# Hybrid decoder block on one core: va, z, gate, branch and output products turned from 256 moving activations to 512 moving weight columns

## The chip, the cores and the metric

One Trainium2 chip, of which the kernel uses one core (core 0). The metric is the device time of one execution in microseconds (us), as a median of several runs. The engines are named as in the profile: PE is TensorE, DVE VectorE, ACT ScalarE, POOL GpSimd, SP the queue that issues most transfers.

## The reference

One decoder block on 256 tokens of 1024 channels, all in float32. Norm weights, the convolution and the decay parameters are left out here.

```python
h = rmsnorm(x, pre_norm_w)
proj = h @ w_in                       # 1024 x 10256
q_a, k_a, v_a, z_a, q_b, k_b, v_b, z_b, beta, decay, gate_a, gate_b = split(proj)
o_a = attention(rope(q_a), rope(k_a), v_a)          # causal softmax, 8 heads of 128
y_a = (o_a * silu(z_a)) @ w_branch_a
q_b, k_b, v_b = split(silu(causal_dwconv(concat(q_b, k_b, v_b))))
o_b = rmsnorm(gated_deltanet(q_b, k_b, v_b, g, beta))   # 8 heads, chunked delta rule
y_b = (o_b * silu(z_b)) @ w_branch_b
merged = sigmoid(gate_a) * y_a + sigmoid(gate_b) * y_b
return x + rmsnorm(merged @ w_out, post_norm_w)
```

With 256 tokens the attention has a single block of keys, so it is plain causal attention.

## The kernel before, in words

**Products.** Every large product is made in three single passes over a split of its operands: each float32 operand is cut into a part `hi` that the fast matmul type (float32r) holds exactly and a rest `lo`, and the product is hi*hi + hi*lo + lo*hi. The weights come as 104 tiles of 512 KB, 128 output columns of all 1024 rows each (`slots`, line 291; `load`, line 319). For each tile `prep` (line 328) has ACT write `hi` (L341), then DVE or, for some tiles, POOL write `lo` (L344 to L346), and then issues the load of the tile five places on, into one of five buffers.

- `projT` (line 376) takes the 128 weight columns as the stationary operand and lets the 256 tokens of the normalised input (`Hh`, `Hl`: hi and lo, channels on partitions) move: 24 matmuls 128x256 for a tile, accumulated in one PSUM tile (`psP`, three of them). The result has channels on partitions, tokens along the row. It serves qb, kb, vb, qa, ka, za, zb, ga, gb and the branch products wa, wb.
- `projN` (line 388) does it the other way for va and the output product wo: 128 tokens stationary, 256 weight columns moving, so a pair of tiles gives two PSUM tiles of 24 matmuls.

**Order of the tiles.** kb, qb, va in pairs; qa, vb, ka in pairs; then eight tiles each of za, zb, ga, gb; then wa and wb in turn; then wo. In what follows dl is the PSUM tile of a head of the delta rule, s that of a head of the attention, kk that of `unit`, vT, oT those of transposes, po that of the output product.

**Order of everything else.** Each engine executes in the order in which the program emits. The tile loop (line 1013) emits the products, and between every three matmuls `tick` (line 198) lets side tasks emit their next stage: `conv` and `unit` (products of a head), `inverses` (DVE: 62 operations on the tile `NtTt`, then a round trip through DRAM as `dT` into the tile `DT`), `head` (the delta rule, starts when `DT` is there), `ybtask`, `att`, `merge`. A stage is emitted when a running estimate of each engine's clock (`clk`, line 60) says that its operands are there; the estimate of a fast matmul is line 128: `max(0.107, size(out) / 2350.0)` us.

**Gates and merge.** `zgate` (line 743) makes z * (1 + tanh(z/2)) by channels. `ybtask` (line 832) scales a head's output per token on DVE, transposes it on PE to channels, gates it from PSUM, and `hilo` (line 819) splits it with ACT and POOL. `att` (line 898) does scores, softmax, transposes of the probabilities, the product with va as the stationary operand, so that its result has channels on partitions, then gate and split. wa and wb then let these tiles move. `merge` (line 948) adds on POOL, and ACT and DVE split into `mH`, `mL`.

**End.** `final` (line 980) is called for each half of the tokens (t) and each 256 columns (n): ACT sums squares, DVE multiplies the PSUM tile by the norm weight; after the last n, eight tiny DVE operations (`ro`) make the reciprocal root, then three DVE (or ACT and POOL) operations add the residual and three transfers write the row.

**Buffers.** `big` has nine tiles of 8 KB a partition, `dp` 24 of 2 KB; PSUM has three banks in `psP` and five in `psM`, which the side tasks take and give back.

Of the kernel before, what the change touches and what calls it, by code (L numbers as in the profile page):

```python
# [37 lines left out]
def tile_moba_gdn_block(  # L38
# [111 lines left out]
    big = ctx.enter_context(tc.tile_pool(name="big", bufs=9))  # L150
    dp = ctx.enter_context(tc.tile_pool(name="dp", bufs=24))
# [21 lines left out]
    left = {"d": [0.0] * 24, "w1": [0.0] * 8, "E": [0.0] * 2}  # L173
# [125 lines left out]

    for n in range(4):  # L300
        pair("kb", KB, n)
        pair("qb", QB, n)
        pair("va", VA, n)
# [13 lines left out]
    raws, wts, natw = {}, {}, {}  # L317

    def load(i, t=None):
        if i < NS:  # L320
            kind, n, src, c0 = slots[i]
            r = wp.tile([P, KT, P], F32, tag="raw", bufs=5, name=f"raw{i}")
            at(clk["T"] if t is None else t)
            dma(nc.sync, r, src.rearrange("(k p) c -> p k c", p=P)[:, :, c0:c0 + P])
            raws[i] = r
            done(f"raw{i}")

    def prep(i, now=False, pool=None):
# [3 lines left out]
        if kind in ("va", "wo"):  # L332
            if (kind, n // 2) not in natw:
                natw[kind, n // 2] = [bigt(f"{kind}{w}{n}", F32R).rearrange("p (k c) -> p k c", k=KT) for w in "hl"]
            c = slice((n % 2) * P, (n % 2) * P + P)
            hi, lo = (a[:, :, c] for a in natw[kind, n // 2])
        else:
            hi = wp.tile([P, KT, P], F32R, tag="hi", name=f"hi{i}")
            lo = wp.tile([P, KT, P], F32R, tag="lo", name=f"lo{i}")
            wts[i] = (hi, lo)  # L340
# [18 lines left out]
    def palloc(name):  # L359
# [6 lines left out]
        ps = psP.tile([P, S], F32, tag="pj", name=name)  # L366
# [9 lines left out]
    def projT(i, rh, rl, name):  # L376
        hi, lo = wts.pop(i)
        ps = palloc(name)
# [9 lines left out]
    def projN(lh, ll, t, wh, wl, name):  # L388
        ps = palloc(name)
        c = 0  # L390
        for k in range(KT):
            for a, b in ((lh, wh), (ll, wh), (lh, wl)):
                T.matmul(ps, a(k)[:, t * P:(t + 1) * P], b[:, k, :], start=(c == 0), stop=(c == 3 * KT - 1))
                c += 1
                if c % 3 == 0 and c < 24:
                    tick()
        return ps

# [65 lines left out]
    first = [palloc(f"pkb{n}") for n in range(2)]  # L464
# [22 lines left out]
    # every product starts as soon as its column and its weights are there  # L487
# [37 lines left out]
    def betadecay():  # L525
# [8 lines left out]
        # beta = 1 / (1 + exp(-b))  # L534
# [3 lines left out]
        # softplus(z) = max(z, 0) + log1p(exp(-|z|))  # L538
# [17 lines left out]
        # cumulative sums over each chunk of 128 tokens, as rows and per token  # L556
# [105 lines left out]
    def factors(g):  # L662
# [10 lines left out]
        # eps * 128 * (|q2|^2 + 4 eps)  # L673
# [66 lines left out]
    zs = [None] * H  # L740
    zsuse = [0] * H

    def zgate(dst, ps, name):
        pid = pids[0] - 1
        th = tmp.tile([P, S], F32, tag="w1", bufs=8, name=f"thz{name}")
        act(th, ps, AF.Tanh, scale=0.5)
        yield
        V.scalar_tensor_tensor(dst, th, 1.0, ps, op0=OP.add, op1=OP.mult)
        pfree(pid)
        free("w1")  # L750
        done(f"z{name}")

# [66 lines left out]
    def hilo(y, src):  # L819
        act(y[:, 0, :], src, AF.Copy)  # L820
        G.tensor_tensor(y[:, 1, :], src, f(y[:, 0, :]), op=OP.subtract)

# [9 lines left out]
    def ybtask(h):  # L832
        yield from need(f"rf{h // 4}", f"zb{h}")
        yield from until(lambda: yrun[0] < 2)
        yrun[0] += 1
        ps = yield from take(f"oT{h}")
        Vs = AV[h][:, 1]
        for t in range(NT):
            u = t * 8 + h
            V.tensor_scalar(Vs[:, t, :], Vs[:, t, :], sm[:, F_, u:u + 1], None, op0=OP.mult)  # L840
        yield
        for t in range(NT):
            T.transpose(ps[:, t * P:(t + 1) * P], Vs[:, t, :], ident)
        yield
        yield from room("w1")
        y = tmp.tile([P, S], F32, tag="w1", bufs=8, name=f"yb_{h}")
        V.scalar_tensor_tensor(y, ps[:, 0:S], gdnw, zs[h][:, 0, :], op0=OP.mult, op1=OP.mult)
        give()
        zsuse[h] += 1
        free("d", 1 + (zsuse[h] == 2))  # L850
        yield from room("d")
        yb[h] = dt_(f"yb{h}", F32R)
        hilo(yb[h], y)
        free("w1")
# [43 lines left out]
    def att(h):  # L898
        yield from need("rope", f"za{h}")
# [19 lines left out]
        V.reciprocal(mx[:, 6:8], mx[:, 4:6])  # L919
        for t, (a, b) in enumerate(ab):  # L920
            V.tensor_scalar(p[:, a:b], p[:, a:b], mx[:, 6 + t:7 + t], None, op0=OP.mult)
        yield
# [3 lines left out]
        act(pe, ps[:, 0:384], AF.Copy)  # L926
        yield
# [5 lines left out]
        y = tmp.tile([P, S], F32, tag="w1", bufs=8, name=f"ya_{h}")  # L933
        V.scalar_tensor_tensor(y, ps[:, 0:256], 0.5, zs[h][:, 1, :], op0=OP.mult, op1=OP.mult)
# [233 lines left out]
```

## Time and profile before

| | |
|---|---|
| median of 3 runs | 405.76 us (404.92 to 408.33) |
| span of the profiled execution | 403.9 us |
| PE busy | 376.6 us, 93% |
| DVE busy | 306.5 us, 76% |
| ACT busy | 199.5 us, 49% |
| POOL busy | 130.6 us, 32% |
| moved by DMA | 64.20 MB, mean 159 GB/s |

The page gives the profiled execution by its span, from the first to the last instruction, and no separate time; the median of the timed runs lies 1.9 us above the span, and that is taken for what lies around it. A busy share is an average over stages. A line of the chain of waits gives start, length and the group that the end was waiting for at that time. A line of the timeline gives the start of the first of a few equal instructions and the time to the end of the last; a matmul's end is modelled and overlaps the next, so the pace of matmuls is read from the distance of starts. All matmuls go through one helper and stand under line 129, transposes under 133, other operations under 117, transfers under 147; they are told apart by tile names.

### The profile page before, as it was taken

To read this page: it belongs to the slowest core of one execution; us is meant where nothing else is said; L and a number is where in the kernel's file an instruction comes from. 1 tells how busy PE (TensorE), PEld (TensorE's weight loads), DVE (VectorE), ACT (ScalarE), POOL (GpSimd) and SP (SyncE) were. 2 spreads that over 40 slices of the span, in tenths; PEclk is the share of its full clock that TensorE was granted. 3 is DMA by queue.
4 is the path that set the end of the run, shared out by engine and by line. 5 is a ranking of instruction groups with operands and counts; after the bars stand their busy time and mean duration, and the time that the engine had idled before them with its cause. 6 is when DMAs were issued, how large, how long until landed. Compare 5 with 4: busy or idle time off the path is not lost.

```text
span 403.9 us, 7830 instructions
## 1 busy us (share of the span) xinstructions
PE 376.6 (93%) x3011; PEld 369.6 (92%) x3011; DVE 306.5 (76%) x664; ACT 199.5 (49%) x429; POOL 130.6 (32%) x102
## 2 busy tenths in 40 slices
PE   6799999959999899789999999999999999999992
PEld 5699999859999899689999999999999999999992
DVE  4869879997959699999966684776988543769645
ACT  3357456534564555435534545654757543444411
POOL 2540447463764453312055001011232201446101
PEclk9699999978999999969999999999999999999998
DMA  8964948543455795346898723342365466577402
GB/s 236 283 157 107 249 132 231 145 133 104 109 154 150 188 286 147 107 126 173 248 288 212 191 57 102 84 102 77 93 169 157 137 195 193 165 229 211 128 0 104
DMA packets 119447, 64.20 MB, mean 159 GB/s; under 512 B 6514, under 2 KB 117987, under 8 KB 119411
## 3 DMA queue, kind: packets, MB, share of 16 engines
q1 hardware_dynamic: 116578, 60.42, 54.8%
q0 software_dynamic: 736, 2.24, 1.6%
q10 hardware_dynamic: 2096, 1.06, 0.9%
q8 instruction: 23, 0.38, 0.4%
q14 instruction: 14, 0.11, 0.1%
HBM read 61.08 MB, written 2.63 MB: 158 GB/s over the span
## 4 chain that ended last, share of the span: by engine, by line
PE 72%; DVE 21%; issue 4%; DMA 1%; ACT 1%; DVEq 0%; SPq 0%; ACTq 0%
PE dl L129 7%; PE po L129 6%; PE pza L129 6%; PE pgb L129 6%; PE pga L129 6%; PE pzb L129 6%; PE pwa L129 5%; PE pwb L129 5%; PE pkb L129 5%; DVE lo L117 4%; DVE NtTt L117 4%; PE pqb L129 4%; PE pvb L129 4%; PE pva L129 3%; PE s L129 3%
## 5 line engine op out<-in xcount | busy, mean ns | idle before, releaser
L117 DVE TENSOR_TENSOR lo<-raw,hi 128x1024 fp32r<-128x1024 f32 x74 | 102.7, 1394 | 10.9 <-ACT hi L117 10.8
L117 ACT ACTIVATE hi<-raw 128x1024 fp32r<-128x1024 f32 x88 | 92.3, 1052 | 19.9 <-PE pwb L129 10.6
L117 POOL TENSOR_TENSOR lo<-raw,hi 128x1024 fp32r<-128x1024 f32 x14 | 34.0, 2432 | 45.7 <-ACT hi L117 45.7
L117 DVE TENSOR_TENSOR NtTt<-NtTt 128x112 f32<-128x112 f32 (+27 forms) x62 | 34.2, 552 | 1.6
L117 POOL TENSOR_TENSOR ya<-ya,ya 128x256 fp32r<-128x256 f32 x8 | 8.5, 1064 | 76.3 <-ACT ya L117 76.3
L117 POOL TENSOR_TENSOR val<-raw,vah 128x1024 fp32r<-128x1024 f32 x8 | 19.6, 2455 | 21.8 <-ACT vah L117 21.8
L129 PE MATMUL pwa<-ya,hi 128*128 128x256 f32 x128 | 23.4, 283 | 0.0
L129 PE MATMUL pwb<-yb,hi 128*128 128x256 f32 x128 | 23.4, 283 | 0.0
L117 POOL TENSOR_TENSOR my<-my,m 128x256 f32<-128x256 f32 x8 | 10.4, 1295 | 33.1 <-DVE my L117 33.1
L129 PE MATMUL pzb<-Hh,hi 128*128 128x256 f32 x64 | 20.8, 325 | 0.0
L129 PE MATMUL pga<-Hh,hi 128*128 128x256 f32 x64 | 20.2, 315 | 0.0
L129 PEld LDWEIGHTS pwb<-yb,hi 128*128 128x128 f32 x128 | 20.0, 192 | 0.0
L129 PEld LDWEIGHTS pwa<-ya,hi 128*128 128x128 f32 x128 | 20.0, 192 | 0.0
L129 PE MATMUL pqa<-Hh,lo 128*128 128x256 f32 x64 | 19.2, 299 | 0.7 <-DVE lo L117 0.7
L129 PE MATMUL pqa<-Hh,hi 128*128 128x256 f32 x64 | 19.7, 308 | 0.0
L129 PE MATMUL pgb<-Hh,hi 128*128 128x256 f32 x64 | 19.2, 300 | 0.0
L129 PE MATMUL pqa<-Hl,hi 128*128 128x256 f32 x64 | 19.1, 299 | 0.0
L129 PE MATMUL pva<-val,Hh 128*128 128x256 f32 x64 | 18.2, 284 | 0.7 <-POOL val L117 0.7
L129 PE MATMUL pkb<-Hl,hi 128*128 128x256 f32 x64 | 18.8, 293 | 0.0
L129 PE MATMUL pkb<-Hh,hi 128*128 128x256 f32 x64 | 18.6, 300 | 0.0
L129 PE MATMUL pwa<-ya,lo 128*128 128x256 f32 x64 | 18.2, 285 | 0.3 <-DVE lo L117 0.3
L129 PE MATMUL pqb<-Hh,hi 128*128 128x256 f32 x64 | 18.3, 286 | 0.0
(375 smaller groups left out, 1438.3 us busy)
## 6 DMA issues: line engine op xcount, KB each, us to landing
raw<-in_w_in_dram SPq DMA_DIRECT2D x80, 512.0 KB, 4.0
raw<-in_w_branch_a_dram SPq DMA_DIRECT2D x8, 512.0 KB, 3.8
raw<-in_w_branch_b_dram SPq DMA_DIRECT2D x8, 512.0 KB, 4.2
raw<-in_w_out_dram SPq DMA_DIRECT2D x8, 512.0 KB, 4.1
Grow<-dg ACTq DMA_DIRECT2D x2, 512.0 KB, 8.3
xr<-in_x_dram POOLq DMA_DIRECT2D x4, 256.0 KB, 4.0
x<-in_x_dram SPq DMA_DIRECT2D x1, 512.0 KB
NtTt<-dN SPq DMA_DIRECT2D x2, 256.0 KB
```

The lines of the kernel that those rows point to most:

```text
L117: LOG(self.e, c, fn(out, *a, **k))
L129: LOG("T", 0, nc.tensor.matmul(out, l, r, **k))
```

## The change

The products va, za, zb, ga, gb, wa, wb and wo all go by tokens: 128 tokens of the activation are stationary, 512 weight columns move, one PSUM bank holds 128 tokens x 512 columns. Their weights come in pieces of 256 rows x 512 columns (512 KB as before), four pieces for a result of 512 columns (`piece`, new `projN`): 12 matmuls for a piece where a tile had 24, first for both halves of the tokens in turn, in the last piece one half after the other. kb, qb, vb, qa and ka stay as they were. va's banks, and those of wo, are taken from `psM` (`mbank`).

z and the gates now lie by tokens. `ybtask` gates and scales by token in one operation, then transposes and splits from PSUM with ACT and DVE. `att` takes the probabilities as the stationary operand, so that its result lies by tokens; it leaves the division by the sum to the gate operation, and transposes and splits afterwards: two transposes more for a head. `merge` adds by tokens on POOL, transposes four blocks on PE for each half of the tokens and 512 columns, and splits from PSUM. POOL's share of the splits of ya, yb and of two wo tiles goes to DVE. `final` works on 512 columns. The estimate of a fast matmul becomes `max(0.12, size(out) / 2370.0)`; `big` has 11 tiles, `dp` 16.

```diff
-            run("T", max(0.107, size(out) / 2350.0) if one else max(0.215, size(out) / 590.0), 0.25)
+            run("T", max(0.12, size(out) / 2370.0) if one else max(0.22, size(out) / 590.0), 0.25)
...
+    def piece(kind, o, c, kk, src=w_in):
+        add(kind, (c, kk), src, o + c * 512)
...
     for k, o in (("za", ZA), ("zb", ZB), ("ga", GA), ("gb", GB)):
-        for n in range(4):
-            pair(k, o, n)
-    for n in range(8):
-        add("wa", n, w_a, n * P)
-        add("wb", n, w_b, n * P)
-    for n in range(4):
-        pair("wo", 0, n, w_out)
+        for c in range(2):
+            for kk in range(4):
+                piece(k, o, c, kk)
+    for c in range(2):
+        for k, src in (("wa", w_a), ("wb", w_b)):
+            for kk in range(4):
+                piece(k, 0, c, kk, src)
+    for kk in range(4):
+        for c in range(2):
+            piece("wo", 0, c, kk, w_out)
...
-        if (kind == "va" and n >= 2 or 24 <= i < 48 and i % 2 == 1 or kind == "wo" and n in (0, 2)) if pool is None else pool:
+        if (kind == "va" and n > (0, 1) or 24 <= i < 48 and i % 2 == 1) if pool is None else pool:
...
-    def projN(lh, ll, t, wh, wl, name):
-        ps = palloc(name)
-        c = 0
-        for k in range(KT):
-            for a, b in ((lh, wh), (ll, wh), (lh, wl)):
-                T.matmul(ps, a(k)[:, t * P:(t + 1) * P], b[:, k, :], start=(c == 0), stop=(c == 3 * KT - 1))
...
+    def projN(i, pss, lh, ll, kk):
+        wh, wl = wts.pop(i)
+        order = [(j, t) for j in range(2) for t in range(NT)]
+        if kk == 3:
+            order.sort(key=lambda e: e[1])
+        for n, (j, t) in enumerate(order):
+            k = 2 * kk + j
+            for m, (a, b) in enumerate(((lh, wh), (ll, wh), (lh, wl))):
+                T.matmul(pss[t], a(k)[:, t * P:(t + 1) * P], b[:, j, :], start=(k == 0 and m == 0),
+                         stop=(k == KT - 1 and m == 2))
...
-    def zgate(dst, ps, name):
...
+    def zgate(dst, ps, pid, then=None):
+        act(dst, ps, AF.Tanh, scale=0.5)
+        yield
+        V.scalar_tensor_tensor(dst, dst, 1.0, ps, op0=OP.add, op1=OP.mult)
         pfree(pid)
...
-        T.matmul(ps[:, 0:256], va[:, 0, hs], pe[:, 0:256], start=True, stop=False)
-        T.matmul(ps[:, 128:256], va[:, 1, hs], pe[:, 256:384], start=False, stop=True)
+        T.matmul(ps[:, 0:128], pe[:, 0:128], va[:, 0, hs], start=True, stop=True)
+        T.matmul(ps[:, 128:256], pe[:, 128:256], va[:, 0, hs], start=True, stop=False)
+        T.matmul(ps[:, 128:256], pe[:, 256:384], va[:, 1, hs], start=False, stop=True)
...
+            T.transpose(ps[:, 256 + t * P:256 + (t + 1) * P], y[:, t, :], ident)
...
-    def merge(n, m, y):
+    def merge(c, t, m, y):
         G.tensor_tensor(y, y, m, op=OP.add)
+        ps = yield from take(f"mT{c}{t}")
         yield
-        act(mH[:, n, :], y, AF.Copy)
-        yield
-        V.tensor_sub(mL[:, n, :], y, f(mH[:, n, :]))
+        for k in range(4):
+            T.transpose(ps[:, k * P:(k + 1) * P], y[:, k * P:(k + 1) * P], ident)
...
+        act(mH[:, ks, ts], pv, AF.Copy)
+        V.tensor_sub(mL[:, ks, ts], pv, f(mH[:, ks, ts]))
```

Where PE first turns to the delta rule (`dl`), it has in the program before done all of za (`pza`) and 21 products of zb (`pzb`):

```order
L129 MATMUL pzb_2629<-Hl,hi_2511 128x256
L129 MATMUL pzb_2629<-Hh,lo_2512 128x256
L129 MATMUL dl_2655<-DT,Mall 128x128 x2
L133 MATMUL dl_2655<-sq,kq_317 128x128
L129 MATMUL dl_2655<-AV_745,DT 128x128
L129 MATMUL dl_2665<-DT,Mall 128x128 x2
```

In the changed program, on the same engine, 93 of the 96 products of za stand ahead of it:

```order
L129 MATMUL pza_2317<-hi_2310,Hh 128x512
L129 MATMUL pza_2317<-hi_2310,Hl 128x512
L129 MATMUL pza_2317<-lo_2311,Hh 128x512
L129 MATMUL dl_2400<-DT,Mall 128x128 x2
L133 MATMUL dl_2400<-sq,kq_317 128x128
L129 MATMUL dl_2400<-AV_707,DT 128x128
L129 MATMUL dl_2410<-DT,Mall 128x128 x2
```

The first `dl` has moved ahead of zb altogether, and the products of 512 columns between ka and it are 93, where there were 213 of 256.

On PE where the output product (`po`) begins, `mT` are the new transposes of the merge. In the changed program they stand behind the first 12 products of wo:

```order
L129 MATMUL po_3871<-hi_3810,mH 128x512
L129 MATMUL po_3871<-hi_3810,mL 128x512
L129 MATMUL po_3871<-lo_3811,mH 128x512
L133 MATMUL mT_3884<-sq,mwb_3864 128x128 x4
L133 MATMUL mT_3889<-sq,mwb_3864 128x128 x4
L129 MATMUL po_3893<-hi_3828,mH 128x512
L129 MATMUL po_3893<-hi_3828,mL 128x512
L129 MATMUL po_3893<-lo_3829,mH 128x512
L129 MATMUL po_3906<-hi_3828,mH 128x512
```

Before, nothing stood between the products of wb and of wo, nor inside wo.

At the end of DVE's program, `ob` is the output row, `ro` and `fo` the reciprocal root. Before, the last rows are:

```order
L117 SCALAR_TENSOR_TENSOR fo<-ro_4823 128x1
L117 SCALAR_TENSOR_TENSOR ob_4629<-ob_4629,fo,xr_4137 128x512
L117 SCALAR_TENSOR_TENSOR ob_4630<-ob_4630,fo,xr_4138 128x256 x2
L117 TENSOR_TENSOR ob_4632<-po_4839,pwt_4142 128x256
L117 TENSOR_REDUCE fo<-fo 128x1
L117 TENSOR_SCALAR fo<-fo 128x1
L117 TENSOR_SCALAR ro_4898<-fo 128x1
L117 TENSOR_SCALAR ro_4898<-ro_4898 128x1 x2
L117 SCALAR_TENSOR_TENSOR ro_4898<-ro_4898 128x1 x5
L117 SCALAR_TENSOR_TENSOR fo<-ro_4898 128x1
L117 SCALAR_TENSOR_TENSOR ob_4631<-ob_4631,fo,xr_4139 128x512
L117 SCALAR_TENSOR_TENSOR ob_4632<-ob_4632,fo,xr_4140 128x256
```

And in the changed program:

```order
L117 TENSOR_TENSOR ob<-po_3893,pwt 128x512
L117 TENSOR_SCALAR ro_4016<-fo 128x1
L117 TENSOR_SCALAR ro_4016<-ro_4016 128x1 x2
L117 SCALAR_TENSOR_TENSOR ro_4016<-ro_4016 128x1 x5
L117 SCALAR_TENSOR_TENSOR fo<-ro_4016 128x1
L117 SCALAR_TENSOR_TENSOR ob<-ob,fo,xr 128x512
L117 SCALAR_TENSOR_TENSOR ob<-ob,fo,xr 128x256 x2
L117 TENSOR_TENSOR ob<-po_3906,pwt 128x512
L117 TENSOR_SCALAR ro_4035<-fo 128x1
L117 TENSOR_SCALAR ro_4035<-ro_4035 128x1 x2
L117 SCALAR_TENSOR_TENSOR ro_4035<-ro_4035 128x1 x5
L117 SCALAR_TENSOR_TENSOR fo<-ro_4035 128x1
```

The rows are the same kinds, but po_3893 and po_3906 are both filled by the last piece of wo, six products apart; before, the first half's last tile was ready two tiles ahead of the end.

## Rows read from the trace of the kernel before

**Rows 1.** The page, busy time of each engine
```profile
PE 376.6 (93%) x3011; PEld 369.6 (92%) x3011; DVE 306.5 (76%) x664; ACT 199.5 (49%) x429; POOL 130.6 (32%) x102
```

**Rows 2.** Busy time by stretch of the whole span
```profile
core 0: us, PE busy (x) PEld busy (x) DVE busy (x) ACT busy (x) POOL busy (x), PEclk, DMA share, GB/s
...
20.00:66.00 46.00, 46.00 (x376) 44.77 (x375) 37.38 (x82) 27.66 (x54) 17.84 (x11) 1.00 0.64 172
66.00:174.00 108.00, 95.41 (x747) 92.98 (x746) 94.50 (x181) 52.29 (x103) 55.90 (x38) 0.96 0.57 152
...
217.30:320.00 102.70, 102.70 (x859) 101.87 (x858) 73.36 (x222) 58.77 (x170) 14.65 (x16) 1.00 0.47 123
320.00:373.20 53.20, 52.83 (x439) 52.42 (x438) 33.98 (x38) 23.93 (x31) 18.07 (x16) 1.00 0.65 192
```

**Rows 3.** Chain of waits: start, length in us, engine, tile, line, count
```profile
185.74 5.76 PE pka L129 x48
...
194.38 0.22 PE vT L133 x2
...
219.60 0.67 PE dl L129 x6
...
231.57 0.66 PE s L129 x4
...
298.94 0.65 PE s L129 x4
...
373.23 23.04 PE po L129 x190
396.29 0.48 ACT jo L117 x2
```

**Rows 4.** Timeline of PE early on: start, us, operation, shape, count
```profile
17.49 0.41 PE L129 MATMUL pkb<-Hl,hi 128*128 128x256 f32 x1
17.70 0.41 PE L129 MATMUL pkb<-Hh,hi 128*128 128x256 f32 x1
...
23.06 0.40 PE L129 MATMUL psbd<-Hh,bdw 128*16 128x256 f32 x2
23.30 0.28 PE L129 MATMUL pkb<-Hh,lo 128*128 128x256 f32 x1
```

**Rows 5.** Busy time by stretch, where PEclk is low; columns as in rows 2
```profile
17.00:18.00 1.00, 1.00 (x7) 0.87 (x5) 0.74 (x3) 0.00 (x0) 0.00 (x0) 0.50 1.02 359
...
76.00:86.60 10.60, 8.68 (x68) 8.16 (x67) 10.39 (x24) 6.26 (x14) 7.20 (x7) 1.00 0.65 172
86.60:93.50 6.90, 4.49 (x19) 4.34 (x20) 4.55 (x19) 1.13 (x2) 0.68 (x1) 0.51 0.59 156
```

**Rows 6.** Tile DT: its issues (first to last start); then DMA issues by line
```profile
L147 SPq DMA_DIRECT2D DT<-dT x4: 481/542/1944, 209.7 to 212.7; - x4
...
dN<-Mall SPq DMA_DIRECT2D x4, 64.0 KB, 3.6
```

**Rows 7.** Groups by line and shape: busy us, mean ns, idle before
```profile
L117 DVE TENSOR_TENSOR lo<-raw,hi 128x1024 fp32r<-128x1024 f32 x74 | 102.7, 1394 | 10.9 <-ACT hi L117 10.8
...
L117 POOL TENSOR_TENSOR rt<-rt,rope 128x512 f32<-128x512 f32 x4 | 7.9, 1973 | 22.8 <-DMA rt<-dq 22.6
...
L117 DVE SCALAR_TENSOR_TENSOR zs<-thza,pza 128x256 f32<-128x256 f32 x8 | 3.3, 417 | 2.0 <-ACT thza L117 2.0
...
L117 POOL TENSOR_TENSOR rt<-rt 128x512 f32<-128x512 f32 x2 | 2.6, 1294 | 0.2
```

**Rows 8.** Timeline of DVE at the end: start, us, operation, count
```profile
391.38 0.20 DVE L117 TENSOR_SCALAR ro<-fo 128x1 f32<-128x1 f32 x1
...
393.35 1.54 DVE L117 SCALAR_TENSOR_TENSOR ob<-ob,fo,xr 128x512 f32<-128x512 f32 x3
...
396.80 0.21 DVE L117 TENSOR_SCALAR ro<-fo 128x1 f32<-128x1 f32 x1 [1.32 <-ACT jo L117]
...
398.99 1.65 DVE L117 SCALAR_TENSOR_TENSOR ob<-ob,fo,xr 128x512 f32<-128x512 f32 x2
```

More of the change, by code (lines that the diff above doesn't have):

```diff
@@ L302, in tile_moba_gdn_block @@
         pair("qb", QB, n)
-        pair("va", VA, n)
+        for j in range(2):
+            piece("va", VA, n // 2, 2 * (n % 2) + j)
     for n in range(4):
@@ L331, in prep @@
         r = raws.pop(i)
[L332 to L340, printed above, removed]
+        shape = [P, 2, 512] if isinstance(n, tuple) else [P, KT, P]
+        hi = wp.tile(shape, F32R, tag="hi", name=f"hi{i}")
+        lo = wp.tile(shape, F32R, tag="lo", name=f"lo{i}")
+        wts[i] = (hi, lo)
         act(hi, r, AF.Copy)
         yield
-        if (kind == "va" and n >= 2 or 24 <= i < 48 and i % 2 == 1 or kind == "wo" and n in (0, 2)) if pool is None else pool:
+        if (kind == "va" and n > (0, 1) or 24 <= i < 48 and i % 2 == 1) if pool is None else pool:
             G.tensor_tensor(lo, r, f(hi), op=OP.subtract)
@@ L365, in palloc @@
             clk["T"] += 0.05
-        ps = psP.tile([P, S], F32, tag="pj", name=name)
+        ps = psP.tile([P, 512], F32, tag="pj", name=name)
         if j >= 0:
@@ L386, in projT, with mbank @@
         return ps
-    def projN(lh, ll, t, wh, wl, name):
-        ps = palloc(name)
-        c = 0
-        for k in range(KT):
-            for a, b in ((lh, wh), (ll, wh), (lh, wl)):
-                T.matmul(ps, a(k)[:, t * P:(t + 1) * P], b[:, k, :], start=(c == 0), stop=(c == 3 * KT - 1))
-                c += 1
-                if c % 3 == 0 and c < 24:
-                    tick()
-        return ps
+    def projN(i, pss, lh, ll, kk):
[8 more added lines that the diff above has]
+                         stop=(k == KT - 1 and m == 2))
+                if m != 1 and n < 3:
+                    tick()
+    def mbank(name):
+        for _ in range(20000):
+            if banks:
+                break
+            tick()
+            clk["T"] += 0.05
+        banks.sort()
+        at(max(banks.pop(0), cur[0]))
+        return psM.tile([P, 512], F32, tag="m", name=name)
     def rsqrt(dst, src, name):
@@ L463, in tile_moba_gdn_block @@
     banks.pop()
-    first = [palloc(f"pkb{n}") for n in range(2)]
+    first = [palloc(f"pkb{n}")[:, 0:S] for n in range(2)]
     def normed(q):
@@ L738, in vnat @@
         done(f"vs{h}")
-    zs = [None] * H
-    zsuse = [0] * H
-    def zgate(dst, ps, name):
-        pid = pids[0] - 1
-        th = tmp.tile([P, S], F32, tag="w1", bufs=8, name=f"thz{name}")
-        act(th, ps, AF.Tanh, scale=0.5)
+    zs = [None, None]
+    def zgate(dst, ps, pid, then=None):
+        act(dst, ps, AF.Tanh, scale=0.5)
         yield
-        V.scalar_tensor_tensor(dst, th, 1.0, ps, op0=OP.add, op1=OP.mult)
+        V.scalar_tensor_tensor(dst, dst, 1.0, ps, op0=OP.add, op1=OP.mult)
         pfree(pid)
-        free("w1")
-        done(f"z{name}")
+        if then:
+            done(then)
     running = [0]
@@ L832, in ybtask @@
     def ybtask(h):
-        yield from need(f"rf{h // 4}", f"zb{h}")
+        yield from need(f"rf{h // 4}", f"zb{h // 4}")
         yield from until(lambda: yrun[0] < 2)
@@ L898, in att @@
     def att(h):
-        yield from need("rope", f"za{h}")
+        yield from need("rope", f"za{h // 4}")
         yield from until(lambda: arun[0] < 3)
@@ L1008, in tile_moba_gdn_block @@
     ahead = {}
     for j in range(6, NS):
-        kind, n = slots[j][:2]
-        if kind != "wo" or n < 6:
-            ahead.setdefault(j - {"wo": 5, "va": 4}.get(kind, 3), []).append(j)
+        ahead.setdefault(j - 3, []).append(j)
+    grp = {}
     for i, (kind, n, src, c0) in enumerate(slots):
@@ L1017, in tile_moba_gdn_block @@
         at(flags[f"w{i}"])
-        if kind == "wa" and n == 0:
-            drain(*[f"y{b}{h}" for b in "ab" for h in range(H)])
         if kind in ("kb", "qb", "vb"):
@@ L1029, in tile_moba_gdn_block @@
                 spawn(conv(ps, 16 + n, v2, f"v{n}", vnat(n, v2)))
-        elif kind in ("zb", "za"):
-            w = 0 if kind == "zb" else 1
-            wait("w1")
-            ps = projT(i, hh, hl, f"p{kind}{n}")
-            if w == 1:
-                wait("d")
-                zs[n] = dt_(f"zs{n}")
-            spawn(zgate(zs[n][:, w, :], ps, kind[1] + str(n)))
         elif kind in ("qa", "ka"):
@@ L1087, in tile_moba_gdn_block @@
         elif kind == "wo":
+            c, kk = n
             mh, ml = (lambda k: mH[:, k, :]), (lambda k: mL[:, k, :])
[L1089 to L1114 removed]
@@ L1115, in tile_moba_gdn_block @@
+            if kk == 0 and c == 0:
+                grp["wo"] = {}
+            if kk == 0:
+                grp["wo"][c] = [mbank(f"po{t}{c}") for t in range(NT)]
+            for t in range(NT):
+                drain(f"mg{kk // 2}{t}")
+                at(max(cur[0], flags[f"mg{kk // 2}{t}"]))
+            projN(i, grp["wo"][c], mh, ml, kk)
+            if kk == 3:
+                for t in range(NT):
+                    final(t, c, grp["wo"][c][t], c == 1)
         tick()
```

229 lines of the change are left out of this document (113 added, 116 removed).

## The prediction, made before the changed kernel ran

> **What bounds the kernel now.** I read the busy times first: PE is busy 93% of the span, DVE 76% [rows 1]. That is an average, so the second view is the busy time by stretch [rows 2]. PE is full from 20 to 66 us and from 217.3 us, the first matmul of dl, to the end of the products; there DVE works 73 of 103 us and is no limit. From 66 to 174 PE is idle 12.6 of 108 us and DVE busy 94.5: here DVE and the transfers it waits for set the pace, and faster products buy little. The third view is the chain of waits [rows 3]. The 48 products of pka take 5.76 us, so a single-pass product with 256 moving columns has a pace of 0.120 us; the last 190 products (po) end at 396.27, and 7.6 us follow, mostly on DVE. So the change is to be judged in three parts: up to the first dl (217.3), from there to the last product (179.0 us), and the tail.
>
> **What one product of 512 columns costs.** No product of this kind stands in the trace. Where the granted clock is 0.50 (1.2 GHz) [rows 5], products of 256 columns start 0.21 us apart [rows 4]: one column a clock and no visible extra. At 2.4 GHz, 256 clocks are 0.107 us, and the pace is 0.120, so 13 ns go elsewhere. Two products with only 16 weight columns also take 0.24 [rows 4], so the number of weight columns is not where they go. What 512 columns cost depends on what the 13 ns are: a floor for one product that longer streaming covers, a fixed extra for each, or a toll on each column. The nearest row is the float32 product, which goes in two passes: six passes of 128 columns in dl take 0.67, so 0.112 each, and a pair s (two passes of 128 and two of 256) takes 0.65 or 0.66, which leaves 0.213 to 0.218 for a pass of 256 columns [rows 3]. 128 columns more cost 0.101 to 0.107 us, two clocks a column, so that pass streams 512 clocks, exactly what the new product needs, at 0.213 to 0.218. I take 0.216. The bounds are 0.213 (512 clocks), 0.227 (13 ns fixed) and 0.240 (twice 0.120).
>
> The Trainium skill (TensorE: Matmul & The Clock Gate, section "Back-to-back issue gap") gives columns / 2.4 + 2.5 ns for warm back-to-back matmuls: 109.2 ns for 256 columns, 215.8 for 512. This rule speaks against the change: the 1,131 products below would go from 123.5 to 124.9 us, no gain at all. At 256 columns the trace differs (0.120), and the trace decides; at 512 no run here shows it yet.
>
> **Part 1, to the first dl: -2.7 us.** Eight tiles of va are 192 products of 0.120 = 23.0 us, now 96 of 0.216 = 20.7. Half of them lie in the stretch where PE is full; of the 2.3 us I count 1.15. From the end of pka at 191.5 PE needed 25.8 us of za, zb and two pairs of vT to reach dl; now it needs 93 x 0.216 + 0.44 = 20.5 [rows 3]. But dl waits for DT. Its last transfer is issued at 212.7 [rows 6]; its landing is not shown; another 64 KB transfer of blocks takes 3.6 us, which puts it at 216.3, 1.0 us ahead of dl. So PE gets there some 5 us earlier and gains 1.0; the rest becomes a wait for DT, behind which everything on PE queues, zb too. DT itself comes at the pace of DVE. Among its 62 operations on NtTt the order has 12 lo and 5 v before, 11 and 4 after, but these two only move ahead of the first NtTt, on the same full engine. Three zs of 0.417 become one operation on 512 columns, at most 0.83 and I take 0.65: -0.6 [rows 7]. Bounds: -8, if the better-timed order removes much of the 12.6 us of PE idling, and +5, if the side tasks miss the two banks that va now holds in psM.
>
> **Part 2, products from dl on: -5.8 us.** Before: 171 of zb, 384 of ga and gb, 384 of wa and wb, 192 of wo, together 1,131 x 0.120 = 135.7 us; the rest of the 179.0 us is delta rule and attention. After: 3 of za, 96 each of zb, ga, gb, 192 of wa and wb, 96 of wo, together 579 x 0.216 = 125.1: -10.6. Added on PE are 16 transposes of ya and 16 of the merge, a pair at 0.22 [rows 3]: +3.5. Attention times va is three products of 128 columns instead of one of 256 and one of 128: as long. PE's idle 0.37 from 320 on [rows 2], a wait that ended with DVE's lo, goes: -0.4.
>
> New waits. A pair of results now takes two of the three psP banks. The next pair's second half starts on the bank of this pair's first half, which is complete 6 x 0.216 = 1.3 us before the last product, and is wanted three products after it: 1.95 us for ACT's tanh and, for z, DVE's operation, about 0.65 each with 512 columns, behind perhaps one hi or lo, a lo being 1.4 [rows 7]. Gates and branches fit; of the four borders of z some run over: +1.0 (0 to 4). The merge: its mT stand behind 12 products of wo, 2.6 us. POOL adds 512 columns in 1.29 to 1.97 [rows 7], two in a row, the first 0.6 us before the last product of wb; the second ends 2.0 to 3.3 us after it, and then mT of the second half goes at 3.05: hardly a wait. But wo's second pair needs mT's bank, which DVE's mL empties behind two lo: +0.7 (0 to 3). DVE is no worse off: with each head it loses two scalings and gains the split of ya and of yb, while POOL loses its part of that work. Sum: -10.6 + 3.5 - 0.4 + 1.0 + 0.7 = -5.8.
>
> **Part 3, the tail: +3.7 us.** Before, DVE is done with the first half's row soon before the last sum of squares; its chain is 7.6 us from the last product to the end. After, both halves end together, and the order on DVE puts all of the first half's work ahead of the second's. From the last product: the first half is complete at -1.3; sum of squares 0.68 (256 columns take 0.48 [rows 3], so 0.48 to 0.96), product with the norm weight 0.68, root 1.97 (391.38 to 393.35), three residual operations 1.54, then the second half's product 0.68, root 2.19, two residual operations 1.65 [rows 8], and 3.26 from there to the end, as from 400.64 to 403.9 before. That is 11.35 against 7.63.
>
> **Sum.** -2.7 - 5.8 + 3.7 = -4.8: the span of 403.9 becomes 399.1. The median of the timed runs is 405.76, 1.9 above that span; the same difference gives **401.0 us**, 1.2% faster. About 1% is what a measurement of this kernel can tell from no change, and 401.7 is that border.
>
> **Rivals.**
> - *512 columns cost twice 256* (slower). If the 13 ns are a toll on columns, the pace is 0.240: part 2 is 579 x 0.024 = 13.9 us worse, va 1.15 on the full stretch, and nothing pays for the transposes and the tail: 416. For it: the float32 passes, which pay 5 ns, take in half as many columns a clock, so they don't exclude it. It gives no gain from 0.224 on, over 1% slower from 0.230. Chance 0.08.
> - *A fixed 13 ns for each product*: 0.227, 6.2 us worse in part 2 and 0.5 in va: 407.7, no change. Chance 0.13.
> - *The wait for DT lets the clock fall.* PE waits 3 to 5 us ahead of dl. Before, it fell to 0.51 from 86.6 to 93.5, after PE had been busy only 8.7 of 10.6 us [rows 5]. Such a stretch at half speed costs 3.4 us: 404.4. The Trainium skill (same page, "HAM oscillation — how this bites in real kernels") describes that fall after waits between bursts, and the trace agrees with its 0.51. Chance 0.12.
> - *Banks.* va's two banks leave side tasks two of five; kk and vT queue, DT comes 4 us later and va's gain goes: about 405. Against it: the order keeps kk at nearly its old places. Chance 0.07.
> - *The planner's better estimate pays more than the width.* It counted 0.109 us for a product that takes 0.120, so it emitted DVE's work for results that were late. With 0.12 a third of the 12.6 us of idling from 66 to 174 may go: 397. Chance 0.20.
>
> **How the numbers follow.** The forecast has 0.40 and a range of its own of 398 to 404, three fifths of it below 401.7: 0.24. With the planner's 0.20 and the fast edges of the others 0.06, faster is 0.50. Slower is the toll 0.08 and the far tails of fixed cost, banks and clock 0.06: 0.14. The remainder, 0.36, is no change. The range 394 to 409 leaves out the toll and the tails.
>
> **What would show it.** Right: starts of pzb or po 0.216 apart; PE idle ahead of the first dl, ended by DT; DVE from last product to end near 11 us. Wrong: starts 0.227 or 0.240 apart; PE waiting for zs, mL or lo in the z stretch; a clock of 0.5 after dl; a first dl later than 217 us.

## The result, and the profile after

The changed kernel takes 418.8 us (median of 4 runs, 416.43 to 421.2); the kernel before takes 405.34 us on the same chip (402 to 410 over all chips used). The ratio is 1.032, with a 95% interval of 1.025 to 1.040. It is slower; the forecast was 401.0 us. Here and below a median is over all runs of a kernel, while a ratio and its interval leave out the runs that met a slower state of the chip.

The profiled execution of the changed kernel is 416.43 us, its span 414.7. The busy times of its page answer to [rows 1]:
```profile
PE 373.2 (90%) x2291; PEld 332.9 (80%) x2291; DVE 293.8 (71%) x641; ACT 197.9 (48%) x396; POOL 104.5 (25%) x76
```
PE is busy 3.4 us less than before, in a span 10.8 us longer: the work did shrink, and idle time took its place. Where it lies is read from the busy time of PE by stretch, up to the first product of wa (334.9 us; before: 326.1). By then both kernels have done the same work: all projections of x, the delta rule and attention. After:
```profile
core 0: us, PE busy (x), PEclk, DMA share, GB/s
20.00:66.00 46.00, 46.00 (x332) 1.00 0.64 181
66.00:130.00 64.00, 54.87 (x375) 0.95 0.46 125
130.00:174.00 44.00, 37.34 (x296) 0.96 0.64 175
174.00:200.00 26.00, 22.31 (x155) 0.87 0.43 134
200.00:240.00 40.00, 36.48 (x199) 1.00 0.77 216
240.00:334.90 94.90, 94.90 (x562) 1.00 0.43 132
sum 314.90, PE 291.89; mean PE 48.65
```
The same stretches of the kernel before:
```profile
66.00:130.00 64.00, 58.33 (x447) 0.95 0.51 134
130.00:174.00 44.00, 37.08 (x303) 0.98 0.66 178
174.00:200.00 26.00, 26.00 (x202) 0.91 0.65 183
200.00:240.00 40.00, 40.00 (x343) 1.00 0.77 204
240.00:326.10 86.10, 86.10 (x714) 1.00 0.44 117
sum 306.10, PE 293.51; mean PE 48.92
```
The last line of each is the reading used for every run below: the length of the stretch from 20 us to the first wa product, and PE's busy time in it. Idle is the difference: 12.6 us before, 23.0 after, and all of the increase lies between 66 and 240 us. What PE waits for, from 60 us on, after:
```profile
engine line waited for: us in total, times, longest us
PE vT L133 <- DVE v L117: 9.2, 3, 4.9
PE psq L129 <- DVE sm L117: 7.1, 1, 7.1
PE pqa L129 <- DVE lo L117: 2.9, 2, 1.8
PE s L129 <- DMA ka<-dq: 1.6, 1, 1.6
PE dl L129 <- DMA DT<-dT: 1.1, 1, 1.1
PE mT L133 <- POOL mwb L117: 0.6, 1, 0.6
PE dl L129 <- ACT kd L117: 0.5, 1, 0.5
PE po L129 <- DVE mL L117: 0.4, 1, 0.4
```
Before, from 60 to 210 us:
```profile
PE vT L133 <- DVE v L117: 5.5, 2, 3.8
PE psq L129 <- DVE sm L117: 4.3, 1, 4.3
...
PE pqa L129 <- DVE lo L117: 0.7, 1, 0.7
```
The three large waits are ones that stood there before, and the three together have grown by 8.7 us. None of them touches a tile that the change made wider. New are the waits for ka and DT behind them. The clock, too, was at its lower level 3.5 us longer between 66 us and the first wa product (17.1 us, before 13.6), which costs half of that.

The chain of waits of the changed kernel shows the pace and the tail, as [rows 3] does for before:
```profile
335.04 10.88 PE pwa L129 x48
...
385.12 17.32 PE po L129 x75
```
48 products of 512 columns take 10.88 us: 0.2267 each. And DVE's timeline at the end, which answers to [rows 8]:
```profile
403.24 0.69 DVE L117 TENSOR_TENSOR ob<-po,pwt 128x512 f32<-128x512 f32 x1 [0.67 <-ACT jo L117]
...
405.81 1.54 DVE L117 SCALAR_TENSOR_TENSOR ob<-ob,fo,xr 128x512 f32<-128x512 f32 x3
407.27 0.68 DVE L117 TENSOR_TENSOR ob<-po,pwt 128x512 f32<-128x512 f32 x1
...
409.83 1.61 DVE L117 SCALAR_TENSOR_TENSOR ob<-ob,fo,xr 128x512 f32<-128x512 f32 x2
```
The second half's product with the norm weight (407.27) stands behind all of the first half's work. From the last product (ended 403.8) to the end of the span are 10.9 us; before, 7.6.

### The profile page after: what moved, and what is told of

Same layout as the page of the kernel before. It is cut to its first block, busy times and chain, and to the rows that moved or that the text cites. A ratio compares the mean times of both kernels' runs of the same rounds, so it can differ in the third digit from the quotient of the medians.

```text
span 414.7 us, 6313 instructions
## 1 busy us (share of the span) xinstructions
PE 373.2 (90%) x2291; PEld 332.9 (80%) x2291; DVE 293.8 (71%) x641; ACT 197.9 (48%) x396; POOL 104.5 (25%) x76
## 4 chain that ended last, share of the span: by engine, by line
PE 69%; DVE 19%; DMA 5%; issue 2%; POOL 2%; ACT 1%; SPq 1%; DVEq 0%; POOLq 0%; ACTq 0%
PE pqb L129 6%; PE pga L129 5%; PE pgb L129 5%; PE pwa L129 5%; PE pwb L129 5%; PE pvb L129 5%; DVE lo L117 5%; PE dl L129 5%; PE pzb L129 4%; PE pqa L129 4%; PE pkb L129 4%; PE po L129 4%; PE pva L129 3%; PE pka L129 3%; PE s L129 3%; DVE rk L117 2%
## 5 line engine op out<-in xcount | busy, mean ns | idle before, releaser
L117 ACT ACTIVATE hi<-raw 128x1024 fp32r<-128x1024 f32 x104 | 109.7, 1056 | 66.4 <-PE pwb L129 13.3
L117 POOL TENSOR_TENSOR lo<-raw,hi 128x1024 fp32r<-128x1024 f32 x22 | 53.6, 2446 | 68.1 <-ACT hi L117 58.7
L129 PE MATMUL pwa<-hi,ya 128*128 128x512 f32 x64 | 19.9, 393 | 0.0
L129 PE MATMUL pwb<-hi,yb 128*128 128x512 f32 x64 | 19.7, 389 | 0.0
L129 PE MATMUL pvb<-Hh,hi 128*128 128x256 f32 x64 | 19.0, 296 | 0.0
L129 PE MATMUL pvb<-Hl,hi 128*128 128x256 f32 x64 | 18.6, 291 | 0.0
L129 PE MATMUL pqb<-Hl,hi 128*128 128x256 f32 x64 | 18.6, 291 | 0.0
L129 PE MATMUL pqb<-Hh,lo 128*128 128x256 f32 x64 | 18.6, 291 | 0.0
L129 PE MATMUL pvb<-Hh,lo 128*128 128x256 f32 x64 | 18.6, 291 | 0.0
L129 PE MATMUL pka<-Hh,hi 128*128 128x256 f32 x64 | 18.2, 284 | 0.0
L129 PE MATMUL pka<-Hl,hi 128*128 128x256 f32 x64 | 18.1, 283 | 0.0
```

What stands on the lines that cost most here:

```text
L117: LOG(self.e, c, fn(out, *a, **k))
```

## The experiments

Ratios are to the kernel before on the same chip, with 95% intervals. The first four ran on one chip, the next four on another, then three, then one.

**The planner's estimate alone, in the kernel before.** The diff also changes a number that only shapes the order: what the planner counts for a product.
```diff
-            run("T", max(0.107, size(out) / 2350.0) if one else max(0.215, size(out) / 590.0), 0.25)
+            run("T", max(0.12, size(out) / 2370.0) if one else max(0.22, size(out) / 590.0), 0.25)
```


> The kernel before with one line of the change alone: the planner's estimate of a fast matmul 0.12 us instead of 0.107 (and size/2370). No product changes. Theory P (the planner's estimate makes part 1 late: side work is emitted earlier against the products than DVE can follow): first dl later than 217.3 by 3 us or more, the first NtTt later than 146.2, time 408 to 412. Theory B (va's two banks in psM make part 1 late): no change, 404 to 407, first dl within 1.5 us of 217.3. My forecast's own rival (the better estimate helps): about 401.

Measured: 414.34 us, 1.017 (1.010 to 1.024). Not one product differs from the kernel before; only the order does. PE by stretch in this run:
```profile
66.00:130.00 64.00, 55.85 (x416) 0.92 0.47 124
...
174.00:200.00 26.00, 21.75 (x171) 0.93 0.55 152
...
sum 316.00, PE 296.37; mean PE 49.39
```
and its waits from 60 to 210 us:
```profile
PE vT L133 <- DVE v L117: 9.2, 3, 4.2
PE psq L129 <- DVE sm L117: 7.6, 1, 7.6
```
These are the two waits of the changed kernel, at nearly the same lengths. Idle is 19.6 us (12.6 before), the clock is at its lower level 6.8 us longer after 66 us (3.4 us lost), and the first wa product starts at 336.0, 9.9 us late. From there to the end it takes 77.8 us, as before. The loss is larger than the 408 to 412 us that was expected, while the first dl, at 219.7, is only 2.4 us late: it stands behind 1,311 large products now and not 1,365, so its start is a poor measure of what was lost.

**The old estimate in the changed kernel** (the same line, the other way).

> The changed kernel with the old estimate line. Theory P: part 1 recovers, first dl near 215 instead of 220.1, PE idle from 66 to 200 us back to some 13 us, time 412 to 414 (the tail and the pace of 0.227 stay). Theory B: first dl stays near 220, time 417 to 420.

Measured: 414.25 us, 1.016 (1.010 to 1.022), so about half of the loss goes. The time is close to what was expected, the way there is not: the first dl starts at 223.9 and not near 215. Idle up to the first wa product (333.2 us) falls from 23.0 to 18.2 us. In its profile PE now stands early, between 59 and 64 us (busy 41.93 of 46 us from 20 to 66, full in every other kernel of that batch), waiting for a lo; with va as before, in the run with all three edits below, it doesn't. PE also waits 2.8 us here for a PSUM bank that DVE's operation on za has to empty.

**va as before in the changed kernel**, with the new estimate.
```diff
-        for j in range(2):
-            piece("va", VA, n // 2, 2 * (n % 2) + j)
+        pair("va", VA, n)
```


> The changed kernel with va alone as before (tiles of 128 columns, 256 moving, psP banks). Theory B: first dl back to 217 or earlier, last kk near 114 instead of 119, time 413 to 415. Theory P: first dl stays near 220 (va itself 1.3 us dearer), time 418 to 421.

Measured: 422.14 us, 1.033 (1.024 to 1.041), with 26.0 us idle up to the first wa product. With the new estimate, va's two banks are not where the time goes; that theory falls. With the old estimate va by itself wasn't tried: the 4.1 us wait for a lo above is there with va wide and gone with va as before, and whether banks or the order of the lo make it is not shown.

**The tail.** The last four weight pieces are multiplied for the first half of the tokens, then for the second.
```diff
-            projN(i, grp["wo"][c], mh, ml, kk)
+            if kk < 2:
+                projN(i, grp["wo"][c], mh, ml, kk)
+            elif kk == 3 and c == 1:
+                for t in range(NT):
+                    for k2 in (2, 3):
...
```


> The changed kernel with the last four pieces of wo done for the first half of the tokens, then for the second, same products. If the tail is 10.9 us because the halves end together, DVE does the first half's row under the last 24 products and the tail falls to 7 to 8.5 us: time 3 us less than the changed kernel's, 415 to 416.5. If the tail is long because of the 512-column operations themselves, it stays above 10 us and the time does not change.

Measured: 417.73 us, 1.021 (1.012 to 1.030); the changed kernel has 1.032. The time is a little above the 415 to 416.5 us expected. The chain ends
```profile
390.93 18.67 PE po L129 x81
...
413.73 0.86 DVEq L1188
```
The last product ends at 409.6 and the span at 417.8: 8.2 us instead of 10.9. The order of the last products costs 2.7 of the 3.3 us by which the tail grew. (Up to wo, PE's order in this run is that of the changed kernel, row for row; yet its first wa product starts at 340.7 us, there at 334.9. Single profiles scatter by that much.)

**All three together**: old estimate, va as before, the last products half by half. Up to the end of pka its order on PE is that of the kernel before.

> The changed kernel with three things put back or moved: the planner's old estimate (0.109 us for a product), va as before (256 moving columns), and the last products of the output half by half of the tokens. Up to the end of pka the order on TensorE is that of the kernel before, row for row. Theory P (the planner's estimate made the products late; width alone is a small gain): pka ends at 191 to 192, the first wa product starts at 323 to 325 (before 326.1: 768 products of 0.120 become 384 of 0.2267, -5.1, and 16 transposes add 1.8), 68.7 from there to the last product as in the two traces with wide products, tail 8.2: span 400 to 402.5, a ratio of 0.990 to 0.997 to the kernel before. Rival W (the wide products with their two banks at a time leave waits of their own in the stretch of the gates): first wa product at 330 or later, as in the run with the old estimate alone (333.2), span 407 or more, ratio 1.007 or more.

Measured: 406.81 us, 1.006 (1.001 to 1.011). Nearly all of the loss is gone, yet the forecast gain of this run isn't there. From its table of stretches:
```profile
200.00:240.00 40.00, 36.87 (x215) 1.00 0.65 193
240.00:328.02 88.03, 88.03 (x516) 1.00 0.43 136
sum 308.02, PE 291.63; mean PE 48.60
```
The first wa product starts at 328.0 instead of 323 to 325; from there to the last product it is 68.9 us (70.2 before), the tail 8.2. From the end of pka to the first wa product it is 137.5 us (134.6 before), where 3.3 less than before was counted: 6.2 us are missing. Half of them are idle time from 200 to 240 us: 3.1 us where before had none (1.4 for DT, 1.0 for ka, 0.7 for kd). DT and ka come from DVE and DMA at their own time, and less of PE's work stands in front of them, the step "the rest becomes a wait for DT" of the forecast. Between pka and the first dl stand 96 wide products (21.8 us), before 213 of 256 columns (25.6): 1.3 of the 3.8 us are the width, the rest is the order. Nor does it take wide products: in the kernel before with the new estimate PE waits 0.8 us for DT and 0.7 for ka. The other half is not idle in the rows: the work of the stretch at its paces (0.2267 for a wide product, 0.109 to 0.112 for a pass or transpose of 128 columns, 0.217 for a pass of 256) sums to 131.8 us, so 2.7 us remain beside the idle time; before, nothing remains. Start times show 1.6 us of it where a side step follows a wide product: 0.252 us behind its start on the mean, from the first dl on (64 places), and not 0.227. A product's modelled end overlaps the next, so a delay this short doesn't show as idle. The saving in the products is spent on both.

**The pace by itself.** No diff: the body is replaced by streams of products.

> This kernel computes no part of the block: its output is the input x, with one stretch of products in its place. It streams products on TensorE back to back: 48 each of single-pass products with 128, 256, 384 and 512 moving columns, a new stationary tile for each product; 48 of 256 and of 512 with the same stationary tile throughout; 24 float32 products each of 128, 256 and 512 columns; 48 in bfloat16 of 256 and of 512. Theory F (a fixed 13.3 ns for every single-pass product): 0.0667, 0.120, 0.173 and 0.2267 us; the float32 product in two passes then 0.112 or 0.120 for a pass of 128 columns. If the fixed part is the change of the stationary tile, the stream with one tile falls to 0.107 and 0.213; if it belongs to the product, it doesn't. Rival (the forecast's 0.216 at 512 columns, a floor that long streams cover): 512 columns in 0.213 to 0.218, and 128 columns well above 0.0667.

Measured, groups by line and shape (busy us, mean ns of one; new: a new stationary tile each time, same: one throughout, both single-pass float32r; full: float32, two instructions for each product; half: bfloat16):
```profile
L73 PE MATMUL new<-xr 128*128 128x128 f32 x48 | 5.5, 274 | 0.0
L73 PE MATMUL new<-xr 128*128 128x256 f32 x48 | 6.0, 284 | 0.0
L73 PE MATMUL new<-xr 128*128 128x384 f32 x48 | 8.5, 335 | 0.0
L73 PE MATMUL new<-xr 128*128 128x512 f32 x48 | 11.1, 390 | 0.0
L73 PE MATMUL same<-xr 128*128 128x512 f32 x48 | 11.1, 390 | 0.0
L73 PE MATMUL full<-x 128*128 128x256 f32 x48 | 10.5, 379 | 0.0
L73 PE MATMUL half<-xb 128*128 128x512 bf16 x48 | 10.5, 379 | 0.0
L73 PE MATMUL half<-xb 128*128 128x256 bf16 x48 | 5.4, 273 | 0.0
L73 PEld LDWEIGHTS full<-x 128*128 128x128 f32 x144 | 23.6, 191 | 12.3 <-issue 11.0
L73 PEld LDWEIGHTS same<-xr 128*128 128x128 f32 x96 | 14.8, 190 | 1.9
```
Busy less one mean, over 47, is the pace; by the start times in the same trace it is 0.112, 0.120, 0.173 and 0.227 us for the float32r products of 128, 256, 384 and 512 columns. Less one column a clock at 2.4 GHz (0.107, 0.160, 0.213) that leaves 13.3 to 13.9 ns at each of the three larger widths: a fixed extra per product. At 128 columns a product takes 0.112 and not the 0.067 of theory F. The extra is not the change of the stationary tile (same: 0.227 too), and of the three types only float32r shows it: a float32 instruction of 256 columns and a bfloat16 product of 512, both 512 clocks, take 0.216. One thing stays open: the stream named same still has a weight load for each product (x96 for its 96 products), so no stream here is without loads, and the extra may be tied to the load. Against that stands the float32 stream, whose loads take as long (191 ns, same: 190) and which has no such extra.

**The estimate, the other way**, in the kernel before: 0.0985 us counted for a product.
```diff
-max(0.107, size(out) / 2350.0)
+max(0.097, size(out) / 2600.0)
```


> The kernel before with one number changed, the other way: the planner counts 0.0985 us instead of 0.109 for a product of 256 columns. Theory P as the order shows it: a larger count puts side work of TensorE behind fewer products (the ninth kk pair behind 345 instead of 381, the first dl behind 1,311 instead of 1,365), so TensorE reaches it before DVE has delivered and stands. With a smaller count there are more products ahead of each: TensorE idles less from 66 to 240 us (12.6 before, 19.6 with 0.12), 8 to 13 us, and the time is 0.98 to 1.00 of the kernel before, unless the side work now comes so late that the delta rule has nothing to hide behind (then 1.00 to 1.02). Rival C (the order is touchy in any direction, 0.109 was found by trial): idle grows to 16 us or more, ratio 1.01 or more.

Measured: 416.17 us, 1.031 (1.026 to 1.036). Idle up to the first wa product is only 14.9 us, but the delta rule now ends so late (the last dl starts at 319 us, before at 279) that nothing is left to hide its waits: 2.8 us for p, 1.9 for AV, and two more stretches at the lower clock, at 326 and 391 us. The expectation allowed for a late delta rule, but for 1.02 at most. Nor does a smaller count simply put more products ahead: the pair of kk that stood behind 381 products stands behind 324, the first dl behind 1,539 instead of 1,365. A change of the estimate costs time in either direction here.

**The new estimate, with DVE, ACT and POOL counted a tenth dearer as well**, in the kernel before.
```diff
-                c = self.cost(op, size(out), a, k)
+                c = 1.10 * self.cost(op, size(out), a, k)
```


> The kernel before with the new estimate of a product (0.12) and the planner's costs of DVE, ACT and POOL all raised by a tenth, so that their ratio to a product is what it was. Theory P (what counts is how many products the planner puts ahead of each side step, so the ratio): the first dl stands again behind some 1,365 products, TensorE idles 12 to 15 us from 66 to 240, ratio 0.998 to 1.005. Rival (the estimate acts in another way, through the releases of buffers and the transfers, which were not raised): ratio 1.012 to 1.02 as with the new estimate alone.

Measured: 412.29 us, 1.018 (1.010 to 1.025). The pair of kk that stood behind 381 products does so again (345 with the new estimate alone), but the first dl stands behind 1,314 and not 1,365; idle is 17.5 us, 6.4 of it psq. So raising these three with the product does not restore the order of before. Transfers and the release of buffers, whose counts were not raised, may be why; that was not tried.

**The new estimate early or late**, in the kernel before: for the first 48 weight tiles (up to ka), or from za on.
```diff
+            new = stage[0] < 48
             if one:
+                c = max(0.12, size(out) / 2370.0) if new else max(0.107, size(out) / 2350.0)
```


> The kernel before with the new estimate of a product only for the first 48 weight tiles (up to the last of ka), the old one from za on. Theory E (the new estimate costs where DVE sets the pace, through the two waits in which TensorE's psq and vT stand for DVE, 3.3 and 3.5 us longer in the run with the new estimate throughout, and the extra 6.8 us of half clock there): ratio 1.012 to 1.020, TensorE idle 17 to 20 us from 20 us to the first wa product. Rival L (the cost comes from za on, where 54 fewer products stand ahead of the first dl): 0.998 to 1.005.

> The kernel before with the old estimate for the first 48 weight tiles and the new one from za on. Theory E: 0.998 to 1.005, TensorE idle 12 to 14.5 us from 20 us to the first wa product, pka ends at 191 to 192. Rival L: 1.010 or more, with the idle time from 190 us on.

Measured: early 414.47 us, 1.019 (1.014 to 1.024); late 408.55 us, 1.007 (1.002 to 1.012). The sums of the two, early first:
```profile
sum 312.44, PE 295.11; mean PE 49.19
```
```profile
sum 306.66, PE 293.47; mean PE 48.91
```
Idle is 17.3 us with the early change (psq 7.6, v 8.1) and 13.2 with the late one, whose profiled execution has a span of 403.8, as before. So the stretch in which DVE sets the pace carries the loss. The late one's ratio is 0.2% above what was expected of no effect; the runs that the ratio rests on scatter from 405.6 to 410.5 us, and what it costs stays open.

**A version built from this**: the kernel before up to zb, with the old estimate; from ga on the changed kernel, with the tail half by half.
```diff
-    for k, o in (("za", ZA), ("zb", ZB), ("ga", GA), ("gb", GB)):
+    for k, o in (("za", ZA), ("zb", ZB)):
+        for n in range(4):
+            pair(k, o, n)
+    for k, o in (("ga", GA), ("gb", GB)):
```


> A version made from what the runs show: the kernel before, with the planner's old estimate, up to the last product of zb (va, za, zb, attention and the delta rule as before; the order on TensorE is that of before, row for row, up to the first product of ga), and from ga on as in the changed kernel (gates, branch and output products by tokens, 512 columns; the merge by tokens and transposed; no transposes of ya), with the last output products half by half of the tokens. By the sums of the runs: gates 384 x 0.120 become 192 x 0.2267, -2.6; from the first wa product to the last product 68.7 instead of 69.9, -1.2; tail 8.4 instead of 7.6, +0.8. Sum -3.0: span 401, ratio 0.990 to 0.996. Rival (any change of the order costs several us, whichever part it is made in): 1.000 to 1.015, with TensorE idle or at half clock between 260 and 330 us.

Measured: 407.69 us, 1.006 (1.002 to 1.009): the rival. From 240 us to the first wa product PE is idle 2.8 us, which it was not before, 2.2 of it at oT:
```profile
240.00:329.21 89.21, 86.44 (x519) 0.98 0.41 128
```
```profile
PE oT L133 <- DVE AV L117: 2.2, 2, 1.8
```

**The same with one more planner's number**: 512 columns counted 0.200 us instead of 0.218, so that the first two oT stand behind 49 and 55 wide products instead of 39 and 40.
```diff
-max(0.107, size(out) / 2350.0) if one
+max(0.107, size(out) / (2350.0 if size(out) <= 256 else 2560.0)) if one
```


> The version of r9_z_narrow with one number changed: the planner counts 0.200 us instead of 0.218 for a product of 512 columns (it takes 0.2267), so that the transposes oT in the stretch of ga stand behind more products (the first two behind 49 and 55 of ga's and gb's instead of 39 and 40). Up to the first product of ga nothing moves. If the 2.8 us of idling between 240 and 330 us in r9_z_narrow (2.2 of it oT waiting for AV on DVE) and the half clock at 288 us are what ate the gain, both go: first wa product at 324 to 326, span 401 to 403, ratio 0.990 to 0.999. Rival (each new order brings waits of its own, and the width is worth no more than they cost): 1.000 to 1.012.

Measured: 402.56 us, 0.992 (0.988 to 0.996). This version beats both kernels. Its stretch of gates:
```profile
240.00:328.66 88.66, 88.66 (x558) 1.00 0.41 124
```
No idle is left there. The profiled execution (406.03 us) is the longest of the twelve, and its first wa product, at 328.7, is later than expected; but the extra time lies ahead of ga, where the order is that of the kernel before. Its chain has
```profile
189.95 5.76 PE pka L129 x48
```
so pka ends at 195.7 and 208.6 us follow to the end of the span of 404.3; before, 212.4 follow (191.5 to 403.9). The 3.8 us between them agree with the ratio. The number 0.200 is further from the true 0.2267 than the one it replaced: it is right for the order, not for the product. Two things stay untested: the same kind of search on the kernel before, with its narrow products, and the wide z in this order.

## Why the prediction was wrong

- **Part 1 (forecast -2.7 us, measured +2.8: the first dl starts at 220.1).** The split into parts is read from one profile each, and those scatter by some us; the ratios over several runs carry the argument. The step that failed is the one on the order. The forecast treated the new estimate as harmless, or, in its last rival, as a gain ("with 0.12 a third of the 12.6 us of idling from 66 to 174 may go"). It has the opposite sign: in the kernel before, that line alone costs 1.7%, and idle rises from 12.6 to 19.6 us. Putting the old line back into the changed kernel lowers its ratio from 1.032 to 1.016. The lower bound of part 1 came from the idea of a gain, the upper one from va's banks; the run with va as before, which keeps the new estimate, is no faster (1.033).
- **The pace (forecast 0.216, measured 0.2267).** The term was mis-sized by taking the float32 pass as the nearest row. The pace run shows that it wasn't near: float32r has a fixed extra of some 13.5 ns, and the float32 instruction doesn't. The rival "a fixed 13 ns for each product" was right, with its price: 579 x 0.0107 = 6.2 us in part 2. The saving there is 1,131 x 0.120 - 579 x 0.2267 = 4.4 us and not 10.6, and the 32 transposes take 3.5 of it. The Trainium skill (TensorE: Matmul & The Clock Gate, section "Back-to-back issue gap") has columns / 2.4 + 2.5 ns; the bfloat16 streams agree (0.109 and 0.216), the float32r ones don't (0.120 and 0.227). By that rule the products gain nothing from width; measured they gain 4.4 us of 135.7, because the extra that the streams show is paid half as often.
- **Waits in part 2.** Forecast 1.7 us (banks of z 1.0, merge 0.7); the rows show 3.3 from the first dl's start on: ka 1.6, mwb 0.6, kd 0.5, mL 0.4, za 0.2. The merge was nearly right (1.0 for 0.7), z's banks were hardly felt (0.2; but 1.0 in the run with the new tail, of the same order up to wo, and 2.8 in the one with the old estimate). The wait for ka, which attention needs, was not in the forecast; it comes with the order as well (0.7 us with the new estimate and narrow products). With the pace this makes 7.8 of the 10.5 us by which part 2 missed (+4.7 against -5.8). The rest, 2.7 us, no row names: PE's idle time is accounted for. By start times 1.8 us of it lie where a side step follows a wide product, 0.269 us behind its start on the mean (47 places) instead of 0.227; before, 63 side steps follow at 0.1205, the pace itself. Such short late starts were a term that the forecast put at nothing.
- **The tail (forecast +3.7, measured +3.3)** was right in mechanism and size, and the run with the last products half by half takes 2.7 of it away.
- **The wait for DT** is there (1.1 us) but short, as PE comes late itself. In the run with the old estimate and va as before, where PE comes early (the first dl at 214.6), it grows to 1.4, with ka and kd behind it. The rival that the clock falls in this wait did not come: from 200 us to the first wa product the granted clock is 1.00 before and after.

Put together: the changed kernel's 1.032 falls to 1.006 when the estimate, the tail and va are put right, and to 1.016 and 1.021 with the first or the second alone. Going by the differences (0.016 and 0.011), these two explain nearly all of it, and va adds nothing that can be seen. What width itself is worth, once its transposes and waits are paid, is little: the versions with z wide and with z as before both stand at 1.006, and wide products from the gates on came to a gain of 0.8%, in an order found by trying a second planner's number. How much of that is the width and how much the order is not shown.

## What to carry to other kernels

Where an order is laid out by estimates, a change of an estimate is an edit of the whole program: time it alone, ahead of the edit that it comes with, and don't expect the truer number to give the better order. A saving on a full engine is worth what is left when the next transfer is due: list the transfers that its work covers, and the short steps that stand behind it, before counting it. And measure the pace of an operation by itself, in the same type, before summing a thousand of them.

## What the runs showed of the hardware

- A float32r product takes one clock a column (2.4 GHz) and about 13.5 ns from 256 columns on, whether its stationary tile is a new one or the same loaded again; 256 columns cost 0.120 us, 512 cost 0.227, and 128 cost 0.112, so going from 256 to 512 saves 5.5% and not 10%. In bfloat16 the extra is 2.5 ns (0.109 and 0.216 us) and there is almost nothing to save. At the clock's lower level no such extra is seen (0.21 us for 256 columns at 1.2 GHz [rows 4]); why, stays open.
- The same order doesn't meet the same clock. The kernel before and the two versions with z as before have the same instructions on PE up to ga, yet the end of pka lies at 191.5, 191.3 and 195.7 us in their profiled executions; the last has two short stretches more at the lower clock, at 77 and 138 us. A difference of 4 us ahead of 200 us in a single profile of this kernel, or of 6 us at the first wa product (334.9 and 340.7 above), proves nothing; the sums of idle time and the intervals over several runs were what decided.
